# Layer norm's scale and bias moved from the reader of the residual rows to their writer, with the bias added by accumulating transfers

## The chip, the cores and the metric

One core of one Trainium2 chip. The metric is the device time of one execution in microseconds (us); the lower, the better.

## What is computed

Four layers over a sequence of 1024 rows of 1024 float32 numbers. Two are hybrid layers (gated delta rule and gated linear attention); two more have an attention (neighbourhood attention in one, grouped-query attention in the other) and a mixture of 32 experts, of which each row takes two. Around each of the six sublayers stands the same frame, cut here to what the change touches:

```python
# hybrid layer
y = jnp.einsum("bte,ed->btd", o, w_out)
x = layer_norm(ALPHA * x + y, ln_g, ln_b)             # (x - mean) * rsqrt(var + eps) * g + b
# layer of the second block
x = layer_norm_2(ALPHA * x + (1 + g1) * (attention @ w_o), ln_g[i, 0], ln_b[i, 0])
h = x * (1 + sc2) + sh2
y = hierarchical_moe(h, ...)
x = layer_norm_2(ALPHA * x + (1 + g2) * y, ln_g[i, 1], ln_b[i, 1])
```

So each normalised row xhat is wanted as a residual, ALPHA * (xhat * g + b), and after the attention sublayers also as the experts' input, xhat * g' + b' with g' = g * (1 + sc2) and b' = b * (1 + sc2) + sh2.

## The kernel before

The rows are cut into 8 tiles of 128 rows (128 x 1024 float32, 512 KB). The kernel is written as many chains (Python generators) with priorities; a list scheduler in the kernel's own code, `Flow`, replays them against modelled clocks and so fixes the order of the instructions on every engine. Nearly all instructions therefore carry the line of the helper that records them, L72; transfers that SyncE (SP) issues carry L185. Working memory is an arena of 47 slots of 128 x 1024.

`out_proj_ln` (called by each hybrid layer and each attention) multiplies the mixer's output with the output weights, tile by tile, adds the residual tile, which `Rows.tile` loads, and calls `finish`: the row statistics and `normalise`, then `Rows.put`, which stores the tile, and `post`. In the hybrid layers `post` transposes the tile for the next layer; in the second block it computes the router's logits, and the normalisation is part of it. For the second block this stage is called the mid stage here, of layer 0 and of layer 1. After its last tile come some hundred small VectorE (DVE) operations, the routing, then an extra block of experts and the experts' loop: per block of rows a gather by an indirect transfer that GpSimd (POOL) issues from the rows of h in DRAM, the three weight matrices, which SP loads, and a scatter that POOL issues and that adds its rows onto Y in DRAM. Each matrix is split in a high and a low part by ScalarE (ACT) and DVE. Layer 0's experts end in `moe_ln`: the second normalisation, a store of the rows, and `N.post`, which feeds the next attention and uses POOL for 64 small subtractions.

`Rows` is the description of such stored rows. Its buffers: xb0 and xb1 after the hybrid layers, xb2 and xb3 for h (x_mid) of layers 0 and 1, Y0 and Y1 for the residual onto which the experts' rows are added, xb4 after layer 0's experts. In `order` listings xb0 is xb_84, xb1 xb_85, xb2 xb_86, xb3 xb_87, xb4 xb_88.

What stands in them differs. xb0, xb1 and xb4 hold xhat; whoever reads a tile multiplies by ALPHA * g and adds ALPHA * b, two POOL operations on 128 x 1024 (`affine`). Y is written with scale and bias already applied (`early=True`): `put` does the same two POOL operations and then stores. For h `put` does a multiplication and an addition on DVE and then stores. The last two tiles of Y are held back until the routing is done (`mid.late`). `prepare` loads g and b at the start of `out_proj_ln`, scales them on ACT and, for h, makes g' and b' with one DVE and three POOL operations.

Of the kernel before, what the change touches and what calls it, by code (L numbers as in the profile page):

```python
# [14 lines left out]
ALU = mybir.AluOpType  # L15
# [17 lines left out]
class Event:  # L33
    def __init__(self):
        self.t, self.value = None, None
# [1435 lines left out]
class Rows:  # L1471
# [1 line left out]

    def __init__(self, x, g=None, b=None, early=False, also=None, mod=None):
        self.x, self.g, self.b, self.early, self.also, self.mod = x, g, b, early, also, mod
        self.rows, self.late = [], None

    def prepare(self, K, user, write=False):  # L1480
        if self.g is None or self.early != write:
            return
        for v in (self.g, self.b):
            r, t = yield from load_rows(K, user, v)
            yield from K.F.until(t)
            K.F.scalar.activation(r.f, r.f, AF.Copy, scale=ALPHA)
            self.rows.append(r)
        if self.mod is not None:
            P = K.F.gpsimd
            sc, t = yield from load_rows(K, user, self.mod[0])  # L1490
            sh, t = yield from load_rows(K, user, self.mod[1])
            g = yield from K.A.take(user)
            yield from K.F.until(t)
# [4 lines left out]
            K.A.give(sh)  # L1498
            self.rows += [g, sc]

    def affine(self, K, x, fast=0):

        P, V = K.F.gpsimd, K.F.vector
        (V if fast > 1 else P).tensor_mul(x.f, x.f, self.rows[0].f)
        (V if fast > 0 else P).tensor_add(x.f, x.f, self.rows[1].f)

    def put(self, K, x, t, user):

        V = K.F.vector
        if self.mod is not None:  # L1510
# [12 lines left out]

    def tile(self, K, x, t):

        F = K.F
        e = F.dma(x.f, self.x[t * 128:(t + 1) * 128, :])
        yield from F.until(e)
        if self.rows:
            self.affine(K, x)  # L1530
        elif not self.early:
            F.scalar.activation(x.f, x.f, AF.Copy, scale=ALPHA)

    def leave(self, K):
        K.A.give(*self.rows)
        self.rows = []


def out_proj_ln(K, oT, outs, wout, rows, eps, after, post, user, prio, freed=None):
# [32 lines left out]
    def finish(t, x):  # L1572
        if t > 1:
            yield posts[t - 2]
        if eps is not None:
            normalise(K, x.f, eps)
        if not after.early:
            yield from after.put(K, x, t, user)
        yield
        yield from post(t, x)  # L1580
        if after.early:
            yield from after.put(K, x, t, user)
        A.give(x)

# [49 lines left out]
        A.give(*o.done.value)  # L1634
    for e in posts:
        yield e
    rows.leave(K)
    after.leave(K)


# [1153 lines left out]
def moe_ln(K, l, Y, last, hold, there, x_out, N, user, prio):  # L2794
# [13 lines left out]
    def one(t, x, e):  # L2808
# [32 lines left out]
    if N is None:  # L2841
# [8 lines left out]
    for e in done:  # L2850
        yield e
    A.give(*hold.half[1].value)
    if N is None:
        A.give(gt, bt)

# [40 lines left out]
def block_2_layer(K, l, X, rows, x_mid, x_out, N, prio):  # L2896
# [21 lines left out]
    mid = Rows(Y, I["ln_g_2"][l, 0], I["ln_b_2"][l, 0], early=True, also=x_mid, mod=mod)  # L2918
    mid.late = M.routed
# [6 lines left out]
def whole(tc, I, O):  # L2926
    with ExitStack() as ctx:
        K = setup(ctx, tc, I)
        setup_2(K)
        xb = [K.dram.tile([S, D], F32, name=f"xb{i}") for i in range(5)]  # L2930

        def main():
            rows, X = yield from first_block(K, I["x"], xb[0:2])
            g, b = I["ln_g_2"][0, 1], I["ln_b_2"][0, 1]
            N = Next(K, "cols2", 0, g, b, 1)
            N.pool = True
            K.A.leave(N.X.user)
            yield from block_2_layer(K, 0, X, rows, xb[2], xb[4], N, 300)
            yield from block_2_layer(K, 1, N.X, Rows(xb[4], g, b), xb[3], O[0], None, 600)

        K.F.spawn(main(), 0)
        K.F.spawn(modulation(K, 90), 145)
        K.F.run()
# [37 lines left out]
```

## Time and profile before

| | |
|---|---|
| Runs | 4152.09, 4154.63, 4155.9 us; median 4154.63 |
| The profiled execution | 4151.23 us, its span 4149.4 us |
| TensorE (PE) busy | 3854.3 us, 93% of the span |
| DVE busy | 3207.2 us, 77% |
| ACT busy | 2194.5 us, 53% |
| POOL busy | 919.6 us, 22% |
| Mean granted TensorE clock | 0.957 of full speed |
| Transfers that SP issues (queue q1) | 644.95 MB |
| Transfers that POOL issues (queue q0) | 33.15 MB |

The profile is one execution. Busy times are sums over the instructions of an engine, so a share of 93% is a mean over stages: some have PE busy throughout, in others PE waits. The stages by time: the hybrid layers to about 1760, the first attention's end and layer 0's mid stage 1795 to 2030, layer 0's experts 2035 to 2640, their end 2639 to 2697, the second attention to 3373, layer 1's mid stage 3373 to 3451, then layer 1's experts.

### The profile page before, as it was taken

The numbers are of one execution on the slowest core, as the hardware profiler recorded it, in microseconds if no ns is written. First come the engines' busy times: TensorE is split into PE (matmuls) and PEld (weight loads), VectorE is DVE, ScalarE is ACT, GpSimd is POOL, SyncE is SP. The second block draws the span as 40 slices with busy tenths as digits, with TensorE's granted clock in tenths as the row PEclk, the third lists the DMA queues.
The fourth block names the chain that finished last, engine by engine and source line by source line (L and its number), as shares of the span: only waits on it lengthen the run. The fifth ranks groups of instructions, "written<-read, shape, count | busy, mean of one in ns | idle before, by whom it ended". The sixth has DMA issues, their size and how long they took to land. (4 is left out here: it accounts for less than half of the span.)

```text
span 4149.4 us, 62801 instructions
## 1 busy us (share of the span) xinstructions
PE 3854.3 (93%) x23000; PEld 3149.1 (76%) x23000; DVE 3207.2 (77%) x5956; ACT 2194.5 (53%) x3931; POOL 919.6 (22%) x638
## 2 busy tenths in 40 slices
PE   7999999999999999979799999889999886999997
PEld 6888788788887777757577777687777775777775
DVE  7787766775777788776789989766657786898898
ACT  4333335433334545441377767667779613777674
POOL 1111100220213233345322221310001251222212
PEclk9999999999999999988799999899999986999998
DMA  4232323111213433243699999400001235999994
GB/s 152 75 100 85 103 77 105 42 38 52 54 57 114 143 120 121 93 135 121 238 354 367 369 367 376 148 11 21 17 25 65 93 111 214 359 367 376 370 362 180
DMA packets 338766, 682.15 MB, mean 164 GB/s; under 512 B 59956, under 2 KB 190702, under 8 KB 338452
## 3 DMA queue, kind: packets, MB, share of 16 engines
q1 hardware_dynamic: 320020, 644.95, 43.2%
q0 software_dynamic: 18432, 33.15, 3.2%
q8 instruction: 182, 2.98, 0.3%
q14 instruction: 132, 1.08, 0.1%
HBM read 625.89 MB, written 86.08 MB: 172 GB/s over the span
## 5 line engine op out<-in xcount | busy, mean ns | idle before, releaser
L72 PE MATMUL banks<-slot 128*128 128x512 f32 (+8 forms) x18258 | 3249.2, 345 | 81.5 <-DVE slot L72 45.5
L72 PEld LDWEIGHTS banks<-slot 128*128 128x128 f32 (+5 forms) x18258 | 2565.3, 178 | 624.9 <-issue 93.1
L72 DVE TENSOR_TENSOR slot<-slot 128x1024 fp32r<-128x1024 f32 (+14 forms) x1417 | 1378.0, 1001 | 129.1 <-ACT slot L72 65.5
L72 ACT ACTIVATE slot<-slot 128x1024 fp32r<-128x1024 f32 (+5 forms) x1011 | 996.5, 1019 | 663.4 <-PE banks L72 233.3
L72 ACT ACTIVATE slot<-banks 128x512 f32<-128x512 f32 (+8 forms) x1124 | 548.7, 510 | 678.0 <-PE banks L72 611.5
L72 POOL TENSOR_TENSOR slot<-slot 128x384 f32<-128x384 f32 (+3 forms) x270 | 451.9, 1692 | 1373.2 <-PE banks L72 404.0
L72 PE MATMUL banks<-c,slot 128*128 128x128 f32 (+2 forms) x3484 | 514.5, 285 | 110.8 <-DVE slot L72 41.8
L72 PEld LDWEIGHTS banks<-c,slot 128*128 128x128 f32 (+1 forms) x3484 | 425.7, 158 | 207.5 <-issue 51.5
L72 DVE TENSOR_TENSOR slot<-banks,slot 128x512 fp32r<-128x512 f32 (+4 forms) x622 | 364.9, 608 | 164.2 <-PE banks L72 92.0
L72 ACT ACTIVATE slot<-slot,small 128x1024 f32<-128x1024 f32 (+1 forms) x292 | 265.9, 923 | 197.5 <-DVE small L72 193.7
L72 DVE COPY slot<-banks 128x512 f32<-128x512 f32 (+6 forms) x406 | 220.2, 551 | 103.4 <-PE banks L72 78.3
L72 POOL MEMSET slot<- 128x1024 f32 (+1 forms) x70 | 66.6, 956 | 836.9 <-PE banks L72 413.8
L72 POOL DMA_INDIRECT Y<-slot,small x62 | 143.5, 2314 | 258.9 <-DVE slot L72 206.3
L72 ACT ACTIVATE slot<-banks,small 128x1024 f32<-128x1024 f32 x140 | 156.5, 1121 | 66.7 <-DVE small L72 58.4
L72 DVE TENSOR_REDUCE small<-banks 128x1 f32<-128x1024 f32 x128 | 154.3, 1220 | 45.2 <-PE banks L72 44.3
L72 PE MATMUL banks<-slot,small 128*128 128x512 f32 (+2 forms) x388 | 158.0, 544 | 19.5 <-ACT small L72 10.2
L72 DVE SCALAR_TENSOR_TENSOR slot<-slot,c_act 128x1024 f32<-128x1024 f32 x84 | 120.0, 1430 | 29.2 <-DMA slot<-in_ada_w 24.2
L72 DVE SCALAR_TENSOR_TENSOR small<-small 128x1 f32<-128x1 f32 (+3 forms) x590 | 128.7, 223 | 12.8
L72 PE MATMUL banks<-small,slot 128*128 128x128 f32 (+1 forms) x576 | 107.0, 301 | 25.0 <-DVE small L72 21.2
L72 ACT ACTIVATE small<-banks 128x64 f32<-128x64 f32 (+2 forms) x289 | 78.0, 274 | 96.9 <-PE banks L72 90.7
L72 DVE TENSOR_TENSOR slot<-slot,banks 128x512 f32<-128x512 f32 (+4 forms) x110 | 72.2, 664 | 69.9 <-PE banks L72 69.0
L72 PEld LDWEIGHTS banks<-small,slot 128*128 128x128 f32 (+1 forms) x576 | 83.6, 200 | 40.4 <-DVE small L72 16.8
(129 smaller groups left out, 1732.7 us busy)
## 6 DMA issues: line engine op xcount, KB each, us to landing
slot<-in_moe_w_up SPq DMA_DIRECT2D x260, 512.0 KB
slot<-in_moe_w_down SPq DMA_DIRECT2D x260, 512.0 KB
slot<-in_moe_w_gate SPq DMA_DIRECT2D x260, 512.0 KB
slot<-in_ada_w SPq DMA_DIRECT2D x96, 512.0 KB
slot<-in_w_in SPq DMA_DIRECT2D x56, 512.0 KB
xb<-slot SPq DMA_DIRECT2D x40, 512.0 KB
slot<-xb SPq DMA_DIRECT2D x24, 512.0 KB
slot<-in_na_w_qkv SPq DMA_DIRECT2D x24, 512.0 KB
```

The lines of the kernel that those rows point to most:

```text
L72: r = real(*a, **k)
```

## The change

The writer now applies scale and bias everywhere, and the reader only loads.

- `prepare` is spawned beside `out_proj_ln` (and beside `moe_ln` of layer 0) and no longer runs ahead of it. It loads g and b, for h also the modulation, which it folds with four DVE operations; ACT scales by ALPHA. Then `preset` fills the destination in DRAM with the bias: the slot that holds b in every row is written to each of the 8 tiles' places by a plain SP transfer.
- `put` multiplies xhat by the scale on DVE, into a slot of its own, and POOL issues a transfer with `accum_op=ALU.add` that adds the slot onto the preset rows. In the mid stages it does so twice per tile, for h and for Y.
- `affine`, `early` and `mid.late` are gone.

In numbers of instructions, from the two listings: POOL loses 86 operations on 128 x 1024 (16 in the second hybrid layer, 35 in each mid stage; the 35 of layer 0 are 16 for the read of xb1, 16 for Y and 3 in `prepare`) and issues 56 accumulating transfers more. DVE loses 34 such operations and gets 64 (56 products and 8 in `prepare`). SP loses 56 stores, and gets 56 presets and 2 more loads of b.

```diff
-            K.F.vector.tensor_scalar(sc.f, sc.f, 1.0 / ALPHA, 1.0 / ALPHA, op0=ALU.mult, op1=ALU.add)
-            P.tensor_mul(g.f, self.rows[0].f, sc.f)
-            P.tensor_mul(sc.f, self.rows[1].f, sc.f)
-            P.tensor_add(sc.f, sc.f, sh.f)
...
-    def affine(self, K, x, fast=0):
-        P, V = K.F.gpsimd, K.F.vector
-        (V if fast > 1 else P).tensor_mul(x.f, x.f, self.rows[0].f)
-        (V if fast > 0 else P).tensor_add(x.f, x.f, self.rows[1].f)
...
+                V.scalar_tensor_tensor(sh.f, b.f, 1.0, sh.f, op0=ALU.mult, op1=ALU.add)
+                V.tensor_mul(b.f, b.f, sc.f)
+                V.tensor_add(sh.f, sh.f, b.f)
+                V.scalar_tensor_tensor(sc.f, sc.f, 1.0, g.f, op0=ALU.add, op1=ALU.mult)
+                self.preset(K, self.also, sh)
+                self.to.append((self.also, sc))
+            t = F.dma(b.f, rows_of(self.b, 0, D))
+            yield from F.until(t)
+        with F.aside():
+            for a in (g, b):
+                F.scalar.activation(a.f, a.f, AF.Copy, scale=ALPHA)
+            self.preset(K, self.x, b)
+            self.to.append((self.x, g))
+        F.set(self.ready)
+
+    def preset(self, K, dst, b):
+        for t in range(NT):
+            K.F.dma(dst[t * 128:(t + 1) * 128, :], b.f)
+        K.A.give(b)

     def put(self, K, x, t, user):
-            with K.F.aside():
-                V.tensor_mul(h.f, x.f, self.rows[2].f)
-                V.tensor_add(h.f, h.f, self.rows[3].f)
-                K.F.dma(self.also[t * 128:(t + 1) * 128, :], h.f)
-                K.A.give(h)
-        if self.late is not None and t >= NT - 2:
-            yield self.late
-        with K.F.aside():
-            if self.early:
-                self.affine(K, x)
-            K.F.dma(self.x[t * 128:(t + 1) * 128, :], x.f)
+        yield self.ready
+        for dst, r in self.to:
+            h = yield from K.A.take(user)
+            with F.aside():
+                F.vector.tensor_mul(h.f, x.f, r.f)
+                F.gpsimd.dma_start(dst[t * 128:(t + 1) * 128, :], h.f, accum_op=ALU.add)
+            def sent(h=h):
+                yield from F.until(F.last(h.f))
+                K.A.give(h)
+            F.spawn(sent(), 0)

     def tile(self, K, x, t):
         e = F.dma(x.f, self.x[t * 128:(t + 1) * 128, :])
         yield from F.until(e)
-        if self.rows:
-            self.affine(K, x)
-        elif not self.early:
+        if self.g is None:
             F.scalar.activation(x.f, x.f, AF.Copy, scale=ALPHA)
...
 def out_proj_ln(K, oT, outs, wout, rows, eps, after, post, user, prio, freed=None):
-    yield from rows.prepare(K, user)
-    yield from after.prepare(K, user, True)
+    F.spawn(after.prepare(K, user), prio - 0.45)
...
 def moe_ln(K, l, Y, last, hold, there, x_out, N, user, prio):
-        F.dma(x_out[t * 128:(t + 1) * 128, :], x.f)
+        if N is None:
+            F.dma(x_out[t * 128:(t + 1) * 128, :], x.f)
+        else:
+            yield from x_out.put(K, x, t, user)
...
+    if N is not None:
+        F.spawn(x_out.prepare(K, user), prio)
```

POOL, layer 0's mid stage up to the first gather (`slot<-xb_86`), as one piece of the difference:

```order
-L72 TENSOR_TENSOR slot<-slot 128x384 x8
-L72 TENSOR_TENSOR slot<-slot 128x1024 x3
-L72 TENSOR_TENSOR slot<-slot 128x384 x6
-L72 TENSOR_TENSOR slot<-slot 128x1024 x2
-L72 TENSOR_TENSOR slot<-slot,small 128x384 x2
-L72 TENSOR_TENSOR slot<-slot 128x1024 x26
...
+L72 DMA xb_86<-slot 128x1024 x2
+L72 DMA Y_15128<-slot 128x1024 x2
+L72 DMA xb_86<-slot 128x1024
+L72 DMA Y_15128<-slot 128x1024
...
 L72 DMA slot<-xb_86,small 128x1024 x2
```

POOL no longer works on the tiles there; in front of the gather stand 16 accumulating transfers, the two of the last tile directly in front of it.

DVE at the end of the first attention, where layer 0's mid stage begins; before:

```order
L72 TENSOR_TENSOR slot<-slot 128x1024
L72 TENSOR_SCALAR slot<-slot,small 128x384
L72 TENSOR_TENSOR slot<-slot 128x1024 x6
L72 COPY slot<-banks 128x384 x2
L72 COPY slot<-banks 128x4x8x16
```

and with the change:

```order
L72 COPY slot<-banks 128x384
L72 TENSOR_SCALAR slot<-slot,small 128x384
L72 COPY slot<-banks 128x384
L72 TENSOR_TENSOR slot<-slot 128x1024 x7
L72 ISA slot,small<-banks,slot 128x384
```

The run of wide operations that splits the output weights is still in one piece, and a copy out of the accumulation banks that stood behind it now stands ahead.

SP behind the extra block of layer 0's experts, before:

```order
L185 DMA slot<-in_moe_w_up 128x1024 x4
L185 DMA slot<-in_moe_w_down 128x1024 x4
L185 DMA slot<-in_moe_w_gate 128x1024 x4
```

and with the change:

```order
L185 DMA slot<-in_moe_w_up 128x1024 x2
L185 DMA slot<-in_moe_w_down 128x1024 x2
L185 DMA slot<-in_ln_g 128x1024
L185 DMA slot<-in_ln_b 128x1024
L185 DMA slot<-in_moe_w_down 128x1024 x2
L185 DMA slot<-in_moe_w_gate 128x1024
L185 DMA xb_88<-slot 128x1024 x8
L185 DMA slot<-in_moe_w_gate 128x1024 x3
```

Two loads and the eight presets of xb4 now stand between the first weights of the experts' loop.

## Rows read from the trace of the kernel before

**Rows 1.** The page of the profile: the span, and its part 1.

```profile
span 4149.4 us, 62801 instructions
...
PE 3854.3 (93%) x23000; PEld 3149.1 (76%) x23000; DVE 3207.2 (77%) x5956; ACT 2194.5 (53%) x3931; POOL 919.6 (22%) x638
```

**Rows 2.** Windows over five stages; columns stand in the first line.

```profile
core 0: us, PE busy (x) PEld busy (x) DVE busy (x) ACT busy (x) POOL busy (x), PEclk, DMA share, GB/s
740.00:780.00 40.00, 33.72 (x155) 27.44 (x155) 32.74 (x60) 19.27 (x28) 13.93 (x8) 0.91 0.05 14
1710.00:1760.00 50.00, 49.71 (x280) 39.62 (x278) 32.36 (x92) 23.72 (x56) 14.26 (x16) 1.00 0.16 56
2178.00:2593.00 415.00, 414.54 (x1861) 330.10 (x1860) 372.16 (x384) 299.96 (x363) 96.21 (x64) 1.00 0.99 370
2639.00:2697.00 58.00, 43.88 (x233) 35.77 (x232) 45.88 (x165) 43.50 (x128) 28.25 (x64) 0.82 0.35 130
3373.00:3451.00 78.00, 46.61 (x275) 40.99 (x273) 72.03 (x185) 12.30 (x19) 39.21 (x17) 0.68 0.45 171
```

**Rows 3.** Groups by shape, POOL: 1795 to 2030, then 3350 to 3455.

```profile
L72 POOL TENSOR_TENSOR slot<-slot 128x1024 f32<-128x1024 f32 x35 | 98.2, 2810 | 73.9 <-DVE slot L72 44.1 <-DMA slot<-xb 27.0 <-issue 1.3
...
L72 POOL TENSOR_TENSOR slot<-slot 128x1024 f32<-128x1024 f32 x18 | 50.3, 2795 | 51.0 <-DVE slot L72 35.8 <-DMA slot<-xb 14.6
```

**Rows 4.** Groups by shape, DVE in the experts' loop, 2178 to 2593.

```profile
L72 DVE TENSOR_TENSOR slot<-slot 128x1024 fp32r<-128x1024 f32 x246 | 289.8, 1219 | 3.2 <-ACT slot L72 0.4 <-PE banks L72 0.3
```

**Rows 5.** Groups by shape, DVE in layer 1's mid stage, 3350 to 3455.

```profile
L72 DVE TENSOR_TENSOR slot<-slot 128x1024 f32<-128x1024 f32 x16 | 34.9, 2198 | 0.0
```

**Rows 6.** Groups by shape, DVE in layer 0's mid stage, 1795 to 2030.

```profile
L72 DVE TENSOR_TENSOR slot<-slot 128x1024 f32<-128x1024 f32 x24 | 36.0, 1503 | 6.7 <-DMA slot<-in_na_w_o 3.6 <-ACT slot L72 3.0
L72 DVE TENSOR_TENSOR slot<-slot 128x1024 fp32r<-128x1024 f32 x8 | 17.4, 2208 | 0.7 <-ACT slot L72 0.7
L72 DVE TENSOR_TENSOR slot<-slot 128x896 fp32r<-128x896 f32 x8 | 13.7, 1721 | 10.5 <-DMA Y<-slot 6.3 <-PE banks L72 3.8 <-ACT slot L72 0.4
```

**Rows 7.** Timelines of DVE, then PE: start, length, operation, idle before.

```profile
1841.88 16.20 DVE L72 TENSOR_TENSOR slot<-slot 128x1024 f32<-128x1024 f32 x6
...
1858.60 5.63 PE L72 MATMUL banks<-slot 128*64 128x128 f32 x40 [15.62 <-DVE slot L72]
```

**Rows 8.** Timeline, end of the routing of layer 1: DVE, then POOL.

```profile
3434.92 1.23 DVE L72 TENSOR_TENSOR slot<-slot 128x1024 f32<-128x1024 f32 x1
...
3437.34 2.31 DVE L72 TENSOR_SCALAR slot<-slot 128x8 f32<-128x8 f32 x1
...
3439.69 0.23 DVE L72 TENSOR_TENSOR slot<-slot 128x64 f32<-128x64 f32 x1
...
3440.20 1.99 DVE L72 TENSOR_TENSOR slot<-slot 128x64 f32<-128x64 f32 x1
...
3450.75 1.08 POOL L72 DMA_INDIRECT slot<-xb,small  x1 [8.64 <-DVE small L72]
```

**Rows 9.** Groups by shape, DVE where xb4 is read, 3264 to 3300.

```profile
L72 DVE TENSOR_TENSOR slot<-slot 128x896 fp32r<-128x896 f32 x4 | 8.4, 2159 | 0.0
L72 DVE TENSOR_TENSOR slot<-slot 128x1024 fp32r<-128x1024 f32 x3 | 7.1, 2366 | 0.0
```

**Rows 10.** The tile Y: POOL's scatters, then all its transfers' landings.

```profile
L72 POOL DMA_INDIRECT Y<-slot,small x62: 2281/2314/2466, 2062.9 to 4085.6; - x62
...
DMA to landing us min/median/max: 4.8/9.7/10.8
```

**Rows 11.** The page's part 3: DMA queues.

```profile
q1 hardware_dynamic: 320020, 644.95, 43.2%
q0 software_dynamic: 18432, 33.15, 3.2%
```

**Rows 12.** Waits of SP's queue in layer 0's experts, 2035 to 2593.

```profile
SPq L185 <- DMA slot<-in_moe_w_down: 130.8, 99, 3.6
...
SPq L185 <- PE banks L72: 86.9, 101, 7.3
```

More of the change, by code (lines that the diff above doesn't have):

```diff
@@ L1471 @@
 class Rows:
[L1476 to L1481, printed above, removed]
-            return
[L1483 to L1487, printed above, removed]
-        if self.mod is not None:
[L1489 to L1493, printed above, removed]
-            K.F.vector.tensor_scalar(sc.f, sc.f, 1.0 / ALPHA, 1.0 / ALPHA, op0=ALU.mult, op1=ALU.add)
-            P.tensor_mul(g.f, self.rows[0].f, sc.f)
-            P.tensor_mul(sc.f, self.rows[1].f, sc.f)
-            P.tensor_add(sc.f, sc.f, sh.f)
-            K.A.give(sh)
-            self.rows += [g, sc]
@@ L1501, in affine, with __init__, prepare @@
-    def affine(self, K, x, fast=0):
-        P, V = K.F.gpsimd, K.F.vector
-        (V if fast > 1 else P).tensor_mul(x.f, x.f, self.rows[0].f)
-        (V if fast > 0 else P).tensor_add(x.f, x.f, self.rows[1].f)
+    def __init__(self, x, g=None, b=None, also=None, mod=None):
+        self.x, self.g, self.b, self.also, self.mod = x, g, b, also, mod
+        self.to, self.ready = [], Event()
+    def prepare(self, K, user):
+        F, V = K.F, K.F.vector
+        if self.g is None:
+            F.set(self.ready)
+            return
+        r = []
+        for v in (self.g, self.b) + (self.mod or ()):
+            r.append((yield from load_rows(K, user, v)))
+        for _, t in r:
+            yield from F.until(t)
+        g, b = r[0][0], r[1][0]
+        if self.mod is not None:
+            sc, sh = r[2][0], r[3][0]
+            with F.aside():
[6 more added lines that the diff above has]
+            t = F.dma(b.f, rows_of(self.b, 0, D))
+            yield from F.until(t)
+        with F.aside():
[3 more added lines that the diff above has]
+            self.to.append((self.x, g))
+        F.set(self.ready)
@@ L1517, in put @@
-        if self.late is not None and t >= NT - 2:
-            yield self.late
-        with K.F.aside():
-            if self.early:
-                self.affine(K, x)
-            K.F.dma(self.x[t * 128:(t + 1) * 128, :], x.f)
+            with F.aside():
+                F.vector.tensor_mul(h.f, x.f, r.f)
+                F.gpsimd.dma_start(dst[t * 128:(t + 1) * 128, :], h.f, accum_op=ALU.add)
+            def sent(h=h):
+                yield from F.until(F.last(h.f))
+                K.A.give(h)
@@ L1528, in tile @@
         yield from F.until(e)
-        if self.rows:
-            self.affine(K, x)
-        elif not self.early:
+        if self.g is None:
             F.scalar.activation(x.f, x.f, AF.Copy, scale=ALPHA)
     def leave(self, K):
-        K.A.give(*self.rows)
-        self.rows = []
+        K.A.give(*(r for _, r in self.to))
+        self.to = []
 def out_proj_ln(K, oT, outs, wout, rows, eps, after, post, user, prio, freed=None):
@@ L1576, in finish @@
             normalise(K, x.f, eps)
-        if not after.early:
             yield from after.put(K, x, t, user)
@@ L1580, in finish @@
         yield from post(t, x)
-        if after.early:
+        if eps is None:
             yield from after.put(K, x, t, user)
@@ L1636, in out_proj_ln @@
         yield e
-    rows.leave(K)
     after.leave(K)
@@ L2852, in moe_ln @@
     A.give(*hold.half[1].value)
+    if N is not None:
+        x_out.leave(K)
     if N is None:
@@ L2917, in block_2_layer @@
     mod = K.mod_d[l][4 * D:5 * D], K.mod_d[l][3 * D:4 * D]
-    mid = Rows(Y, I["ln_g_2"][l, 0], I["ln_b_2"][l, 0], early=True, also=x_mid, mod=mod)
-    mid.late = M.routed
+    mid = Rows(Y, I["ln_g_2"][l, 0], I["ln_b_2"][l, 0], also=x_mid, mod=mod)
     user.peak = 39
@@ L2937, in main @@
             K.A.leave(N.X.user)
-            yield from block_2_layer(K, 0, X, rows, xb[2], xb[4], N, 300)
-            yield from block_2_layer(K, 1, N.X, Rows(xb[4], g, b), xb[3], O[0], None, 600)
+            after = Rows(xb[4], g, b)
+            yield from block_2_layer(K, 0, X, rows, xb[2], after, N, 300)
+            yield from block_2_layer(K, 1, N.X, after, xb[3], O[0], None, 600)
         K.F.spawn(main(), 0)
```

3 lines of the change are left out of this document (1 added, 2 removed).

## The prediction

> **What bounds the kernel now.** I begin with the page: PE is busy for 93% of a span of 4149.4 us [rows 1]. That is a mean, so the next view is the windows, cut by stage [rows 2]. In the experts' loop (2178 to 2593) PE is busy for 414.54 of 415 us: nothing taken from another engine can shorten it, and the transfers, at a share of 0.99, have no room. The end of the second hybrid layer (1710 to 1760) is full of PE as well, 49.71 of 50. Layer 1's mid stage (3373 to 3451) is not: PE 46.61 of 78, DVE 72.03. There DVE sets the pace, and half of its time is not its own work. The groups by shape show that: a DVE operation with two slots as inputs takes 1.22 us on 128 x 1024 in the experts' loop, where POOL does none of `affine`'s [rows 4]; in this stage, where POOL runs 18 operations of 2.80 us [rows 3], 16 of the same size take 2.20 us each [rows 5]. In layer 0's mid stage POOL runs 35 of 2.81 us [rows 3], and three DVE groups are long as well [rows 6]. So POOL's row operations, off the path by themselves, stretch DVE's where DVE is the path. The timelines show one such place whole: six wide DVE operations take 16.20 us, and PE stands idle for 15.62 until DVE's next copies come [rows 7].
>
> **Layer 1's mid stage.** POOL's 18 operations go, DVE's 16 stay 16: a product and an addition for h become two products. The excess is 16 x (2.198 - 1.219) = 15.7 us [rows 4, 5]. DVE is busy for 72.03/78 of the stage [rows 2], so 14.5 of it lie on the path. In the routing two operations of a few columns take 2.31 and 1.99 us beside Y's last two tiles, where one of this kind takes 0.23 [rows 8]: 3.9 us more, all of it on the path to the gather. Together 18 us gained. Bounds: 0, if PE's work or the transfers end last instead, and 78 - 46.6 = 31, if only PE's work were left.
>
> **Layer 0's mid stage.** The excess in the three groups is 24 x 0.284 = 6.8, 8 x 0.99 = 7.9 and 8 x 0.65 = 5.2 us (the last against 1.219 x 896/1024 = 1.07) [rows 4, 6]: 19.9 us, most of it beside PE's work. On the path lies the gap: six operations at 1.22 us are 7.3 us, so 8.9 of the 16.20 go [rows 7]; the change leaves this run of DVE in one piece (seven). With the routing's 3.9, taken as in layer 1 (an estimate), I gain 13. Bounds: 4, if the gap only moves to a later run of DVE, and 24, the whole excess.
>
> **The read of xb4.** Seven DVE operations are long beside `affine`: 3 x 1.15 + 4 x 1.09 = 7.8 us [rows 4, 9]. Nothing shows that DVE ends that stage alone: bounds 0 and 7.8, and I take 3.
>
> **The hybrid layers.** `affine` also leaves the second hybrid layer, and 8 DVE products (8 x 1.22 = 9.8 us) come into the end of each. At the end of the second, PE hides them [rows 2]: nothing, and up to 5 us lost if its 0.3 us of room were no cover for a late transpose. At the end of the first (740 to 780) PE and DVE are busy for 33.72 and 32.74 of 40 us [rows 2]; the transposes don't wait for the product, only for the engine behind it: 1 us lost, bounds 0 and 5.
>
> **The end of layer 0's experts.** Here 8 products (9.8 us) come to a DVE that is busy for 45.88 of 58 us, and 8 issues to a POOL that is busy for 28.25 with subtractions on which the next products of PE rest [rows 2]. POOL's scatter with addition takes 2.31 us to issue [rows 10], its plain gather 1.08 [rows 8]: 8.6 to 18.5 us on POOL, which still fits into the stage. Neither engine becomes full, but the tile's chain passes through both. I take a third to a quarter of the 28 us together: 6 us lost, bounds 2 and 12. What speaks against the change here: POOL's issues could be held up by DVE. The scatters are issued beside a DVE that is busy for 372 of 415 us [rows 2], and none of 62 takes over 2.47 us [rows 10]. The Trainium skill's page SBUF — State Buffer, section 🔬 SBUF: two separate sides, says that a transfer issued from GpSimd starves for descriptors while VectorE holds the shared port; its section on the wrong bandwidth intuition gives some 3.1 us instead of 0.62. By that figure the 8 issues would be 24.8 us (an estimate), and my 6 would be 8; the rows here show nothing so long, and the sum goes by them.
>
> **The weight stream of layer 0's experts.** Ten transfers of 0.524 MB (two loads, eight presets) stand between the first weights on SP's queue, 10 x 0.524 MB at 370 GB/s = 14.2 us [rows 2]. Is this stream hidden? SP waits longer for transfers that hold a slot (130.8 us for one matrix alone) than for PE to free one (86.9) [rows 12], so it runs not far ahead. Yet PE is busy throughout. I take 3.5 us lost, bounds 0 and 14.2. The presets of the mid stages replace stores one for one, in a stage with DMA at 0.45 [rows 2]: nothing, covered by that idle half; behind them on SP's queue stand the first weights, and these are in place long before the gather.
>
> **The gather.** It must wait until both accumulating transfers of the last tile have landed; before, its own rows were a plain store. The scatter, of the same kind and on average 33.15 MB/128 = 0.26 MB [rows 11], lands in 9.7 us, at most 10.8 [rows 10]. A tile is twice that. By the queue's mean a tile's transfer costs 0.524 x (0.032 x 4149.4 us/33.15 MB) = 2.1 us of all 16 engines, a plain one 1.5 [rows 11], so I add 3 us of transfer: 12 to 13 us. The room: the last tile's product for h ends at 3436.15, and the gather goes out at 3450.75 [rows 8]; of these 14.6 us the routing's 3.9 fall away, which leaves 10.7. So each of the two gathers is 2 us late, 4 lost; bounds 0 and 9.7 for each, the last if one more scatter's time lies ahead of it.
>
> **The sum.** Gained 18 + 13 + 3 = 34; lost 1 + 6 + 3.5 + 4 = 14.5; net 19.5. The profiled execution of 4151.2 us becomes 4131.7. The median of the runs lies 3.4 above that execution, so the predicted time is **4135 us**. A measurement of this kernel tells about 0.2%, 8.3 us, from no change: faster is below 4146.3, slower above 4162.9.
>
> **The rivals.** *The whole excess comes through.* If layer 0's mid stage gives 24 us and layer 1's 24 (its small operations are stretched too), the xb4 read 6, and the losses halve to 7, the net is 47; with half of these extras 33. That is 4108 to 4122, middle 4115. For it: DVE is the stage's engine, at 72.03 of 78. Against: in layer 0 only one gap of this size stands between PE's work. 13%.
>
> *Gained in the mid stages, given back at the experts.* The ten transfers cost their 14.2 us because the weights have no room at a DMA share of 0.99 [rows 2], the end of layer 0's experts costs 10, the gathers 6: 34 - 31 = 3, which is 4152. For it: SP's waits [rows 12]. Against: PE's 414.54 of 415 says that the stream still arrives in time. 18%.
>
> *Slower: the gather waits for the accumulating transfers.* If these queue behind one another (16 per stage on one queue) and behind the weights that SP has begun to load, the last lands L us after its product, and each stage loses L - 10.7. Without the gathers the net gain is 23.5, so it is used up at L = 22.5; over 0.2% is lost from L = 26.6. At L = 30, three of the landings of [rows 10], it is 38.6 lost against 23.5 gained: 4154.6 + 15 = 4170. For it: POOL's issues are in order, and a transfer that reads and writes DRAM has no row of this size. Against: 8 tiles in 78 us come some 10 us apart, and DMA is at 0.45. 14%. That the change doesn't do what it says is no case here: the listing shows all 86 POOL operations gone.
>
> **How the numbers follow.** The forecast has 55%, with 4125 to 4143 as its own range. The rival that gains more has 13%; both lie below 4146.3, so faster has 68%. Given back is the 18% of the same, the late gather the 14% of slower. The range of 8 in 10 reaches from 4105, below the rival that gains more, to 4160, past the one that gives all back; what it leaves out is the late gather and a few per cent below.
>
> **What would show it.** Right: wide POOL operations only outside the mid stages, DVE's of 128 x 1024 at about 1.22 us there, PE's gap of 15.62 down to some 7, the stage from the last attention product to layer 1's gather shorter by 16, and PE still busy throughout the experts' loop. Wrong: a gather that a transfer releases, tens of us after the last DVE product; PE gaps in the first rounds of layer 0's experts, where the presets stand; an end of layer 0's experts over 12 us longer, with POOL's issues well above 2.3 us each; or mid stages as long as before, with another engine full.

## The result, and the profile after

The changed kernel takes 4097.66 us (median of 4 runs, 4093.67 to 4102.15), the kernel before 4155.26 in the same session: a ratio of 0.9866, 95% interval 0.9848 to 0.9885. Run once more beside later experiments it took 4109.41 (4094.53 to 4112.13), a ratio of 0.9883 (0.985 to 0.9916); so two sessions of one kernel can lie 12 us apart. Against the forecast of 4135 and its range from 4105 the sign is right and the size is not: 58 us gained, and not 20.

The page of the changed kernel, span, engines and POOL's DMA queue:

```profile
span 4098.2 us, 62930 instructions
...
PE 3826.4 (93%) x23000; PEld 3123.1 (76%) x23000; DVE 3145.8 (77%) x5986; ACT 2207.1 (54%) x3931; POOL 756.7 (18%) x608
...
q0 software_dynamic: 26496, 62.51, 7.4%
```

PE is busy for 28 us less than before [rows 1] with the same 23000 instructions, POOL for 163 us less; POOL's queue now moves 62.51 MB and not 33.15 [rows 11].

To see where 51 us of span went, cut both traces where the same number of matmuls is done. Windows of the kernel before (length, then PE, PEld, DVE, ACT, POOL busy with their counts, the granted clock, DMA share, GB/s): the end of the first hybrid layer, layer 0's mid stage up to its first gather (905 matmuls), layer 1's with the read of xb4 ahead (825):

```profile
680.00:800.00 120.00, 112.41 (x520) 91.94 (x519) 91.53 (x245) 56.15 (x110) 19.34 (x12) 0.96 0.21 60
1795.00:2026.00 231.00, 175.47 (x905) 142.94 (x903) 171.64 (x408) 50.00 (x88) 108.97 (x47) 0.81 0.36 128
3264.00:3450.00 186.00, 145.12 (x825) 122.07 (x824) 147.41 (x303) 34.82 (x48) 83.79 (x32) 0.84 0.36 128
```

The changed kernel: the same three (518, 905 and 820 matmuls), and then pieces of layer 0's experts and of their end, which answer to two of [rows 2]:

```profile
676.00:808.00 132.00, 112.97 (x518) 90.84 (x517) 94.81 (x256) 61.43 (x130) 25.48 (x19) 0.92 0.30 65
1815.00:1994.00 179.00, 154.73 (x905) 125.89 (x904) 138.54 (x408) 50.69 (x87) 29.31 (x26) 0.93 0.75 221
3234.00:3386.00 152.00, 134.69 (x820) 113.65 (x818) 102.15 (x307) 32.35 (x45) 15.80 (x18) 0.92 0.77 218
2145.00:2560.00 415.00, 410.18 (x1837) 324.98 (x1836) 371.26 (x381) 304.27 (x359) 98.26 (x62) 1.00 0.99 370
2606.00:2664.00 58.00, 39.52 (x196) 30.16 (x194) 55.82 (x171) 38.33 (x108) 32.67 (x55) 0.82 0.54 113
```

Read as a ledger, with the starts and lengths of these windows: layer 0's mid stage begins 20 us later than before (1815 against 1795), 12 of them lost at the end of the first hybrid layer (132 against 120). It is 52 us shorter (179 against 231). Layer 1's window begins 30 earlier, so layer 0's experts and their end gave 2 back. It is 34 shorter (152 against 186). The end comes 51 earlier, so layer 1's experts and what follows gave 13 back. 20 - 52 + 2 - 34 + 13 = -51. Eight of the 51 are luck of the execution: after 3500 matmuls, at about 560 us, where the work is still almost the same, the profiled execution of the changed kernel is 8.0 us ahead of the kernel before. The profiled execution of its repeat is 0.2 us behind there and ends 39 us ahead.

In layer 0's mid stage the 905 matmuls kept PE busy for 175.47 us before and 154.73 now: a granted clock of 0.81 against 0.93, 21 us. The other 31 are PE's idle time. DVE does 408 operations in both, in 171.64 and 138.54 us.

DVE's groups of the changed kernel, two rows of layer 1's stage behind those of layer 0's; they answer to [rows 5, 6]:

```profile
L72 DVE TENSOR_TENSOR slot<-slot 128x1024 f32<-128x1024 f32 x25 | 29.9, 1218 | 2.8 <-ACT slot L72 2.8
...
L72 DVE TENSOR_TENSOR slot<-slot 128x1024 fp32r<-128x1024 f32 x8 | 9.6, 1224 | 2.5 <-ACT slot L72 2.4
L72 DVE TENSOR_TENSOR slot<-slot 128x896 fp32r<-128x896 f32 x8 | 8.6, 1084 | 2.1 <-ACT slot L72 2.1
...
L72 DVE TENSOR_TENSOR slot<-slot 128x1024 f32<-128x1024 f32 x18 | 21.6, 1221 | 3.8 <-ACT slot L72 3.6
L72 DVE SCALAR_TENSOR_TENSOR small<-small 128x1 f32<-128x1 f32 x56 | 10.9, 195 | 1.9
```

All wide operations stand at the undisturbed duration of [rows 4]. The last row is the surprise. The same one-column operations of layer 1's stage, before, then two runs of seven of them, and what POOL does beside the second run:

```profile
L72 DVE SCALAR_TENSOR_TENSOR small<-small 128x1 f32<-128x1 f32 x56 | 18.9, 338 | 1.7
...
3344.64 1.50 DVE L72 SCALAR_TENSOR_TENSOR small<-small 128x1 f32<-128x1 f32 x7
3354.53 4.89 DVE L72 SCALAR_TENSOR_TENSOR small<-small 128x1 f32<-128x1 f32 x7
...
3353.69 4.87 POOL L72 TENSOR_TENSOR slot<-slot 128x1024 f32<-128x1024 f32 x2 [14.61 <-DMA slot<-xb]
```

They read two operands of 4 bytes in each partition and still lost 8 us in all, but not evenly: 51 of the 56 took at most 224 ns, as 55 do in the changed kernel, and five took 1.45 to 2.26 us. Each of these five ended 15 to 23 ns after a product of POOL that had begun before it. In layer 0's stage none took over 0.87 us, and their sum is nearly the same before and after, 11.0 and 10.8 us.

PE's gap behind the run of wide DVE operations in layer 0's mid stage, then its longest gap there, at the routing; then the way to layer 1's gather, DVE's last product but one and POOL's last two issues (start, length, idle before):

```profile
1847.12 0.90 PE L72 MATMUL banks<-c,slot 128*128 128x128 f32 x3 [5.80 <-DVE small L72]
...
1987.64 0.19 PE L72 MATMUL banks<-both,before_b 128*128 128x32 bf16 x1 [8.50 <-DVE both L72]
...
3374.13 1.23 DVE L72 TENSOR_TENSOR slot<-slot 128x1024 f32<-128x1024 f32 x1
...
3375.65 0.87 POOL L72 DMA_DIRECT2D xb<-slot  x1 [5.98 <-DVE slot L72]
3376.93 0.87 POOL L72 DMA_DIRECT2D Y<-slot  x1 [0.41 <-DVE slot L72]
3386.57 1.74 POOL L72 DMA_INDIRECT slot<-xb,small  x1 [8.78 <-DVE slot L72]
```

The gap at the routing, before:

```profile
2019.95 0.19 PE L72 MATMUL banks<-both,before_b 128*128 128x32 bf16 x1 [13.06 <-DVE both L72]
```

The gap of 15.62 us [rows 7] became one of 5.80, that of 13.06 one of 8.50. The gather is released by DVE, not by a transfer; the last accumulating transfer was issued 9.6 us before it.

### The profile page after: what moved, and what is told of

Same layout as the page of the kernel before. It is cut to its first block, busy times and chain, and to the rows that moved or that the text cites. A ratio compares the mean times of both kernels' runs of the same rounds, so it can differ in the third digit from the quotient of the medians.

```text
span 4098.2 us, 62930 instructions
## 1 busy us (share of the span) xinstructions
PE 3826.4 (93%) x23000; PEld 3123.1 (76%) x23000; DVE 3145.8 (77%) x5986; ACT 2207.1 (54%) x3931; POOL 756.7 (18%) x608
## 3 DMA queue, kind: packets, MB, share of 16 engines
q0 software_dynamic: 26496, 62.51, 7.4%
HBM read 626.94 MB, written 115.44 MB: 181 GB/s over the span
## 5 line engine op out<-in xcount | busy, mean ns | idle before, releaser
L72 PE MATMUL banks<-slot 128*128 128x512 f32 (+9 forms) x18258 | 3231.3, 343 | 81.9 <-ACT slot L72 55.6
L72 DVE TENSOR_TENSOR slot<-slot 128x1024 fp32r<-128x1024 f32 (+13 forms) x1445 | 1360.0, 964 | 245.1 <-ACT slot L72 168.2
L72 POOL TENSOR_TENSOR slot<-slot 128x384 f32<-128x384 f32 (+2 forms) x184 | 225.6, 1251 | 982.3 <-PE banks L72 416.8
L72 POOL DMA_DIRECT2D xb<-slot x40 | 35.1, 885 | 725.2 <-DVE slot L72 581.3
L72 DVE SCALAR_TENSOR_TENSOR small<-small 128x1 f32<-128x1 f32 (+3 forms) x590 | 120.1, 211 | 11.7
```

The lines of the kernel that those rows point to most:

```text
L72: r = real(*a, **k)
```

## The experiments

Several variants come from one file in which each buffer of rows can be switched between the old and the new manner (`old=True` brings back `affine`, the plain store and, for the mid stages, the hold on Y and the blocking preparation). For comparison, the two mid stages, cut in every trace from the same matmul (the 905th before layer 0's first gather, the 822nd before layer 1's) to the start of that gather: the length, PE's idle time in it and DVE's busy time, in us.

```text
kernel      layer 0: length, PE idle, DVE   layer 1: length, PE idle, DVE   median, all runs
before      231.1  55.3  171.7              186.4  41.6  147.8              4153 to 4156
changed     179.3  24.4  138.8              153.1  17.9  103.3              4097.7, 4109.4
e_dummy     209.4  42.3  168.6              179.6  39.0  137.8              4163.3
e_memset    179.3  24.8  139.8              149.4  15.3  103.8              4107.2
e_read      202.3  37.5  159.8              174.3  28.6  121.0              4136.7
e_write     213.1  36.0  161.6              161.1  22.5  117.6              4132.1
e_spawn     223.8  53.1  178.3              178.7  35.5  137.6              4152.5
e_dve       192.6  30.7  169.3              162.6  26.0  131.1              4101.1
e_plain2    179.4  23.7  138.7              147.2  14.5  103.2              4083.7
```

**e_dummy and e_memset: is it POOL's reading?** Both add POOL work to the changed kernel whose results nobody uses, in a small tile of its own; the order on the other engines stays, but for some twenty rows.

```diff
+def idle(K, x):                       # e_dummy
+    for _ in range(4):
+        K.nc.gpsimd.tensor_mul(K.idle, x.f[:, 0:448], x.f[:, 448:896])
+def idle(K, x):                       # e_memset
+    K.nc.gpsimd.tensor_mul(K.idle[:, 0:8], x.f[:, 0:8], x.f[:, 8:16])
+    for _ in range(10):
+        K.nc.gpsimd.memset(K.idle, 0.0)
...
+            if rows.reads:
+                idle(K, w[0])
             yield from rows.tile(K, x, t)
...
         yield self.ready
+        if self.mod is not None:
+            idle(K, x)
```

> The changed kernel with POOL work put back in both mid stages that nobody waits for: per tile four products of 448 columns beside the read of the residual tile and four beside the writes (64 per stage; 98 us of wide operations stood there before). The order on PE, DVE, ACT and SP stays that of the changed kernel but for some twenty rows. Theory P (POOL's row operations block DVE, PE starves, its clock falls; that is where the mid stages' gain of some 80 us came from): most of the gain goes again, 4130 to 4160 us, DVE's wide operations in the mid stages well above 1.22 us. Theory C (the chain of each tile became shorter: no two POOL operations between load and addition, prepare no longer ahead, Y not held back): within 8 us of the changed kernel's 4097.7.

> The control to e_dummy: the same places in POOL's order, but each group of four products is one product of 8 columns and ten fills of 448 columns, which write to SBUF and read nothing from it; POOL is about as long busy. Theory P (POOL's reads of SBUF block DVE's operations with two inputs there): within 10 us of the changed kernel's 4097.7, DVE's products at 1.22 us. Theory Q (what costs in e_dummy is POOL's queue: accumulating transfers issued late, slots held longer): as e_dummy, 4150 to 4165.

Measured: e_dummy 4163.34 us, ratio to before 1.0023 (1.001 to 1.0037): the time is that of the kernel before, and a little more. e_memset 4107.2, ratio 0.9898 (0.9857 to 0.9939): the gain stays. The groups of layer 0's mid stage, first e_dummy, then e_memset (both lines of POOL's added work and DVE's wide products):

```profile
L1476 POOL TENSOR_TENSOR idle<-slot 128x448 bf16<-128x448 f32 x64 | 101.0, 1578 | 31.0 <-ACT slot L72 27.5
L72 DVE TENSOR_TENSOR slot<-slot 128x1024 f32<-128x1024 f32 x25 | 37.4, 1515 | 2.0 <-ACT slot L72 2.0
```

```profile
L1477 POOL MEMSET idle<- 128x448 bf16 x160 | 82.7, 517 | 8.3
L72 DVE TENSOR_TENSOR slot<-slot 128x1024 f32<-128x1024 f32 x25 | 29.9, 1217 | 2.9 <-ACT slot L72 2.9
```

With 101.0 us of POOL's products DVE's take 1.515 us; with 82.7 us of its fills, 1.217. So it is POOL's reading of SBUF that stretches DVE's operations, not its being busy and not its queue. The Trainium skill, SBUF — State Buffer, section Who interferes with whom, says just this: a DVE instruction with two SBUF inputs contends with a GpSimd instruction that reads SBUF, not with one that only writes it. Both runs agree with it, 1.515 against 1.217 us.

In the mid stages, though, e_dummy takes back 30 us of 52 and 27 of 33, together 57 of 85, with DVE busy nearly as long as before. Some 28 us stay gained. No run says whether they have another source or whether the added products only meet DVE's work in other places than the old ones did. Nor is e_dummy quite without a wait: ACT waits for the added products for 19.9 us (two waits) in layer 0's stage, but PE's waits on ACT come to 3.9 us there, against 1.5 in the changed kernel.

**e_read and e_write: which side?** `mid` in the old manner and the rest new; and the reverse.

```diff
-OLD = ()
+OLD = ("mid",)                  # e_read
+OLD = ("xb0", "xb1", "xb4")     # e_write
```

> Mid stages write h and Y as before (POOL operations, plain stores, Y's last tiles held back, prepare ahead); xb0, xb1 and xb4 as in the changed kernel, so that the readers have no POOL operations. Theory P: read and write shares add up by their POOL time (16 of 35 operations each stage), so 0.45 of the mid stages' 80 us is gained and the losses outside (some 27 us) stay: 4142 to 4152. Theory C with the read side alone deciding: 4100 to 4110.

> Only the mid stages as in the changed kernel (presets, products, accumulating transfers); xb0, xb1 and xb4 as before, with the readers' POOL operations. Theory P: 0.55 of the mid stages' 80 us without the losses outside: 4105 to 4120. Theory C with the write side alone deciding: below 4090. If the read side decides: above 4135.

4136.71 us (0.9956, 0.9939 to 0.9973) and 4132.11 (0.9948, 0.9932 to 0.9964), both outside what theory P gave. In the mid stages the two sides add up. Readers: 28.8 and 12.1 us less than before; writers: 18.0 and 25.3; together 84, and the changed kernel has 51.8 + 33.3 = 85. Outside, e_read keeps the hybrid layers' loss and e_write the one in the experts' loops, so the medians show less.

**e_spawn: the preparation.** The kernel before, with both preparations beside the projection; readers and writers wait for theirs.

```diff
     if rows.old:
-        yield from rows.prepare_old(K, user)
+        F.spawn(rows.prepare_old(K, user), prio - 0.45)
     if after.old:
-        yield from after.prepare_old(K, user, True)
+        F.spawn(after.prepare_old(K, user, True), prio - 0.45)
```

> The kernel before with its two preparations beside the output projection and not ahead of it; POOL's row operations, stores and the hold on Y's last tiles stay. Theory C (the blocking preparation cost the mid stages their time): over 15 us faster than before. Theory P: within 8 us of before, 4147 to 4163.

4152.48 us, ratio 0.9992 (0.9972 to 1.0012): nothing in the whole. In its trace, an execution of 4170.93 us, the two mid stages are 7.3 and 7.7 us shorter than before, and the way to layer 0's stage 31 us longer. So the preparation may account for part of the 28 us that e_dummy leaves; one trace doesn't show it.

**e_dve: the work stays, the engine changes.** The kernel before, with `affine` on DVE.

```diff
     def affine(self, K, x):
-        P = K.F.gpsimd
+        P = K.F.vector
```

> The kernel before with the row operations of readers and of Y on DVE and not on POOL (three POOL operations of each preparation stay). Every instruction's work is as before, the engine alone differs. Theory P: DVE gets 32 operations of 1.22 us in each mid stage, 39 us, and loses some 30 to 37 us of stretching there; so within 25 us of before, 4130 to 4180, and DVE's wide operations at 1.22 us. Without blocking (rival) it would be 39 us per mid stage slower where DVE sets the pace: above 4200.

4101.1 us (4087.16 to 4108.08), ratio 0.986 (0.9834 to 0.9886): as fast as the changed kernel, by one word. Both theories expected less. DVE's wide operations in layer 0's mid stage:

```profile
L72 DVE TENSOR_TENSOR slot<-slot 128x1024 f32<-128x1024 f32 x56 | 69.1, 1260 | 3.7 <-DMA slot<-in_na_w_o 3.7
```

There are 56 now where [rows 6] has 24, at 1.260 and not 1.503. The work added to DVE is 32 x 1.22 = 39 us, and the stage is still 38 us shorter than before, with DVE busy for 169.3 us against 171.7. So the long chain of presets, products and accumulating transfers is not what the gain rests on, and the sum of DVE's busy time is not what sets the stage's length. What sets it is where PE waits: its idle time fell from 55.3 to 30.7 us. That POOL's two slow steps also left each tile's chain, in this run as in the changed kernel, is a rival that e_dve doesn't tell from the stretching; e_dummy, which stretches DVE's operations without those steps, takes back only 57 of the 85. In the mid stages e_dve gains 62 us of the 85; it has no wait on the gate in layer 1's experts (see e_pool).

**e_plain2: what the addition costs.** The order of every engine is that of the changed kernel; the transfers overwrite, so the bias is missing from the rows.

```diff
-                F.gpsimd.dma_start(dst[t * 128:(t + 1) * 128, :], h.f, accum_op=ALU.add)
+                F.gpsimd.dma_start(dst[t * 128:(t + 1) * 128, :], h.f)
```

> The changed kernel with every engine's order unchanged, but the POOL transfers of the rows overwrite and do not add; the bias of the layer norms is left out of the rows that way (the presets are still written). Theory A (adding in the transfer costs nothing that PE sees: landing 5.6 us, and the gathers wait for the routing): within 6 us of 4097.7. Rival (the read and write of DRAM delays slots or gathers): over 10 us faster.

4083.71 us (4082.2 to 4087.36; 0.9832, 0.9811 to 0.9852), some 14 below the changed kernel and 26 below its repeat: theory A falls, though the intervals of the ratios still touch (0.9848 for the changed kernel). POOL's transfers of rows (count, KB each, us to landing), the changed kernel and then this one:

```profile
xb<-slot POOLq DMA_DIRECT2D x40, 512.0 KB, 5.6
...
Y<-slot POOLq DMA_DIRECT2D x16, 512.0 KB, 8.8
```

```profile
xb<-slot POOLq DMA_DIRECT2D x40, 512.0 KB, 3.9
...
Y<-slot POOLq DMA_DIRECT2D x16, 512.0 KB, 5.5
```

An addition lands 1.7 to 3.3 us later. In layer 0's mid stage nothing follows from it. Layer 1's is 6 us shorter, 147.2, but 149.4 in e_memset, which adds in its transfers. Most of the time is saved in the hybrid layers: 6 us of PE's idle time at the end of the first, where slots come free sooner, and 5.5 at the start of the first attention.

**e_xb0old, in_rows, e_best12: the hybrid layers.** The changed kernel loads the second hybrid layer's first weights late. Its SP queue, the first split that waits for them, PE's gap behind it, and SP's waits from 600 to 700 us (total, times, longest):

```profile
699.35 7.83 SPq L185 DMA_DIRECT2D slot<-in_w_in  x3
...
710.45 1.06 ACT L72 ACTIVATE slot<-slot 128x1024 fp32r<-128x1024 f32 x1 [7.64 <-DMA slot<-in_w_in]
...
718.44 1.22 PE L72 MATMUL banks<-slot 128*128 128x512 f32 x2 [11.69 <-ACT slot L72]
...
SPq L185 <- DMA xb<-slot: 15.0, 2, 7.6
```

The same load before:

```profile
679.28 1.01 SPq L185 DMA_DIRECT2D slot<-in_w_in  x2
```

Every product holds a slot until its transfer has landed, and SP has none for the weights. e_xb0old stores xb0 as before (`OLD = ("xb0",)`). in_rows multiplies xb0, xb1 and xb4 in place, behind the transposes. e_best12 is in_pool12 (below) with xb0 as before and its reader on DVE.

```diff
+def INPLACE(rows):                       # in_rows
+    return rows.mod is None
...
-            h = yield from K.A.take(user)
+            h = x if INPLACE(self) and dst is self.x else (yield from K.A.take(user))
...
             normalise(K, x.f, eps)
-            yield from after.put(K, x, t, user)
         yield
         yield from post(t, x)
-        if eps is None:
-            yield from after.put(K, x, t, user)
-        A.give(x)
+        yield from after.put(K, x, t, user)
+        if not INPLACE(after):
+            A.give(x)
```

> The changed kernel with only the first hybrid layer's rows (xb0) as before: xhat stored plainly, the second layer's reader multiplies and adds on POOL. Theory S (the slots that products hold until their accumulating transfers land delay the next layer's weight loads on SP, and PE waits 11.7 us at 718): 12 to 16 us faster than the changed kernel, 4082 to 4086, and no wait of PE above 4 us between 690 and 740. Rival (the POOL operations come back at the read in the second layer and cost there what they cost in the mid stages): within 5 us of 4097.7.

> The changed kernel with xb0, xb1 and xb4 multiplied in place after the transposes; nothing of the planner's constants changed, and the order in layer 1's experts' loop is that of the changed kernel. Theory S (slots held by the accumulating transfers delay the next layer's weights): 12 to 17 us faster than the changed kernel, 4080 to 4086. Rival (what PE gains there it loses at the next wait): 4094 to 4101.

> As in_pool12, but xb0 is stored plainly as xhat, as before, and the second hybrid layer's reader multiplies and adds on DVE, not on POOL. Theory H (the changed kernel's loss in the hybrid layers comes from the slots of the first layer's accumulating transfers; e_xb0old gave none of it back because POOL's reading returned in the second layer): within 4 us of in_pool12, since in place already freed the slots. Rival (any transfer of rows with addition in the first layer costs, in place too): 5 to 12 us faster than in_pool12.

e_xb0old: 4108.21 us (0.9882, 0.9861 to 0.9903), no gain. in_rows: 4091.36 (4089.57 to 4110.14; 0.9863, 0.9832 to 0.9894), its profiled run 4089.57. e_best12: 4088.16 (0.9841, 0.9813 to 0.9868), not faster than in_pool12. PE's waits from 640 to 780 us in in_rows:

```profile
PE banks L72 <- DVE slot L72: 6.1, 2, 5.3
PE banks L72 <- ACT slot L72: 1.0, 2, 0.5
```

and in the repeat of the changed kernel, where the wait on the split comes again:

```profile
PE banks L72 <- ACT slot L72: 14.7, 3, 11.3
```

So the slots cause that wait: 14.7 us, twice, and 1.0 in place. e_plain2, with the changed kernel's order and landings 1.7 us sooner, has 9.3. The profiled execution of in_rows reaches layer 0's mid stage at 1796.5 us, that of the changed kernel at 1814.8. That this is worth 12 us or more in the whole time the medians don't show: 4091 against 4098 and 4109.

Why e_xb0old gained nothing is open in part. It passes the end of the first layer (matmuls 4300 to 4500) in 56.1 us, the changed kernel in 68.2, so the 12 us are there. Its profile loses 6 of them again where a stretch of 20 us at half clock follows a gap of 2 us at 930; the kernel before has the same gap and loses less. It loses 9 more between matmuls 8000 and 8500, where xb0 is read on POOL again: 120.6 us, with PE idle for 10.2, against 112.0 and 2.2. e_best12, which reads on DVE there, takes 111.8; but the kernel before, with its POOL operations, takes no more, 110.7. POOL's reading alone is therefore not shown as the cause.

**e_pool, in_pool12 and the repeats: the order in layer 1's experts.** The changed kernel's loop has a wait of PE per expert that the kernel before has not. PE's waits there (total, times, longest), before and changed:

```profile
PE banks L72 <- ACT small L72: 0.5, 2, 0.2
```

```profile
PE banks L72 <- ACT small L72: 9.9, 21, 0.5
```

The engine is ACT: the gate's activation stands behind one more split of weights. The planner's arithmetic decides that, so one constant was changed.

```diff
-        return 1.04        # what the planner reckons for the issue of a POOL transfer
+        return 0.87        # e_pool; with in_rows e_inpool
+        return 1.2         # with in_rows: in_pool12
```

> The changed kernel with one constant of the planner changed: what it reckons for the issue of a POOL transfer, 1.04 us, is 0.87, as measured on the accumulating ones. POOL's and SP's order stay; on ACT the activation of the gate in layer 1's experts' loop comes one split earlier, which is the order that the kernel before had. Theory O (that order costs PE 0.47 us per expert, 10 us in all): 4085 to 4091 us, and PE's waits on that activation fall from 9.9 us to under 1. Rival (PE waits for something else in the same place, the weights for one): 4094 to 4101.

> As e_pool, and the rows xb0, xb1 and xb4 are multiplied in place, after the transposes, so that their accumulating transfers hold no slot of their own. Theory S (slots held by these transfers delay the next layer's weights on SP; 11 us of PE's idle time at 718 and some 5 at 1390): 4070 to 4080 us. Rival (SP's order still has those weights behind the last tile of the input, so PE waits as long): as e_pool, within 5 us.

> As in_rows, and the planner reckons 1.2 us for the issue of a POOL transfer (not 1.04), which brings back, in layer 1's experts' loop, the repeating order on ACT and DVE that the kernel before had, the weights' splits four ahead of the gate. Theory O (it is this lead that decides PE's wait per expert: 0.47 us at a lead of 0, 3.1 at 1, none at 4): PE's waits in that loop under 1.5 us, 4068 to 4078. Rival (the wait has another cause, such as the gather): within 4 us of in_rows or slower.

> in_pool12 once more, beside the changed kernel on the same chip: 12 to 20 us faster than that one.

> The changed kernel once more, for the comparison on one chip: 4093 to 4104 us; PE's 0.47 us per expert in layer 1's loop again, and its idle time at the end of the first hybrid layer again 10 us or more above the kernel before, if both are matters of the order and not of this execution.

e_pool: 4209.51 us, 112 slower than the changed kernel, with POOL's and SP's order as it was; e_inpool: 4207.25. in_pool12: 4080.9 (0.9829, 0.9795 to 0.9863), again 4083.01 beside 4109.41 for the changed kernel. The waits on the gate, e_pool and in_pool12:

```profile
PE banks L72 <- ACT small L72: 60.7, 20, 5.3
```

```profile
PE banks L72 <- ACT small L72: 0.2, 1, 0.2
```

Theory O had the place right and e_pool's direction wrong: a truer constant made the wait 3 us per expert, a less true one removed it. From layer 1's gather to the end PE idles for 78 us more in e_pool than in the changed kernel and loses 36 more at half clock, which accounts for the 112. in_pool12 is the fastest version found, 15 to 26 us below the changed kernel, although its layer 0 mid stage is longer, 194.9 and 187.5 us in its two profiles. The repeat of the changed kernel, at 4109.41, lies above the 4104 expected of it; its trace has the 9.9 us on the gate again, and the wait at the end of the first hybrid layer.

## Why the prediction was wrong

**The bound and the mechanism: right, and shown for two thirds of the mid stages' gain.** POOL's row operations stretched DVE's, PE waited for DVE, and without them DVE's wide operations stand at 1.22 us. e_dummy and e_memset show that POOL's reading costs 57 of the 85 us. That these operations were "off the path by themselves" is not shown: for the other 28 us it stays open whether POOL's slow steps in each tile's chain, the preparation that ran ahead or the new order counted, or whether e_dummy's products stretch less than the old ones.

**Layer 0's mid stage: 13 forecast, 52 measured. This is the step that failed.** "19.9 us, most of it beside PE's work. On the path lies the gap" took one gap out of a stage, with the routing, and called the rest covered. The two places that it counted came nearly as forecast: the gap gave 9.8 us for 8.9, the wait at the routing 4.6 for 3.9. Two terms were missing. First, the other waits: of PE's idle time 31 us went, so 17 more than in these two places (PE's waits on DVE's slots came to 29.0 us before and to 1.2 now). Second, the granted clock: at 0.81 before and 0.93 now the same 905 matmuls take 21 us less. The sum had no line for what PE's waits cost at half clock. DVE's excess was larger than counted as well: its 408 operations became 33 us shorter, and not 19.9 + 3.9. Narrower operations that the sum left out make up the rest, those of 128 x 384 for one; here before and after:

```profile
L72 DVE TENSOR_SCALAR slot<-slot,small 128x384 f32<-128x384 f32 x16 | 9.9, 626 | 0.0
```

```profile
L72 DVE TENSOR_SCALAR slot<-slot,small 128x384 f32<-128x384 f32 x16 | 6.6, 426 | 0.0
```

**Layer 1's mid stage and the read of xb4: 21 forecast, 34 measured.** The same two terms: PE's busy time is 10 us shorter and its idle time 24; DVE's busy time is 45 shorter (303 and 307 operations), where the sum counted 15.7 + 3.9 + 7.8 = 27. Eight of these 45 are the one-column operations.

**The gather: 2 us late each forecast, not late at all.** The term took the scatter's 9.7 us and added 3; the rows land in 5.6 and 8.8, and DVE releases the gather. POOL's issue was mis-sized as well, in the same direction:

```profile
L72 POOL DMA_DIRECT2D xb<-slot x40: 857/866/1213, 632.6 to 3375.7; - x40
```

It takes 0.87 us, below the lower end taken, 1.08. The Trainium skill, SBUF — State Buffer, section 🔬 SBUF: two separate sides, lets such issues starve for descriptors while VectorE runs an operation in a 2-port mode; the prediction weighed that at 3.1 us each. Nothing of it shows in this trace: none of the 40 issues took over 1.213 us. The slower rival, which rested on late landings, had no ground.

**The experts of layer 0 and their end: 9.5 us lost forecast, 2 measured.** PE is busy for 410.18 of 415 us, so the presets and the loop's order cost under 5 us, where the term had 3.5. The end of the stage lost little, though DVE is busy for 55.82 of 58. The term itself was misreckoned: a third to a quarter of its 28 us is 7 to 9, and not 6.

**The hybrid layers: 1 us lost forecast, 20 measured.** The step "the transposes don't wait for the product, only for the engine behind it" looked at engines and not at slots. Some 12 lie at the end of the first layer, where PE waits for weights that found no slot. Another 7 lie around 1391, at the start of the first attention, where PE has a gap of 9.91 us; in_rows idles there as long, so its cause stays open. The 20 are net of the 8 us of luck in the first 560: the repeat, without them, arrives at layer 0's mid stage 29 us late.

**Layer 1's experts and the end: nothing forecast, 13 lost.** Some 10 of it is the wait on the gate. The prediction took a loop that is full of PE as safe from the change; a different start of the loop gave it another repeating order.

The rival in which "the whole excess comes through" was nearest, at 4115, and its conditions (24 us in each mid stage) were still too small. That it came near is in part luck: by the ledger the mid stages gained 86 us, and 35 were lost elsewhere.

## What to carry to other kernels

Where GpSimd works on rows beside a VectorE that TensorE waits for, don't price the stretch on the wide operations and the visible gap alone: narrow ones, down to one column, can wait for the end of a GpSimd product too. Add what TensorE then loses at half clock: cut the trace by equal numbers of matmuls and read idle time and busy time apart. The sum of VectorE's busy time is no forecast of the stage (e_dve). Then try the cheapest way to take the reading off GpSimd; one word (e_dve) gave as much as the change. In a kernel whose order a planner writes, look at the repeating order of the longest loop after every edit, since there one place in a queue times 32 is worth more than most edits.

## What the runs showed of the hardware

- GpSimd's products hold up VectorE's operations of one column: five of 56 took 1.45 to 2.26 us and ended 15 to 23 ns after the product, the others at most 0.22. Fills by GpSimd left VectorE's wide products at 1.217 us.
- An accumulating transfer of 512 KB lands in 5.6 to 8.8 us, a plain one by the same queue in 3.9 to 5.5, and its issue takes 0.87 us. With the same bytes, GpSimd's queue takes 7.4% of the 16 DMA engines' span with the additions and 5.0% without (e_plain2). The page counts as much read from HBM with the additions as without, 626.94 MB.
- Executions of one kernel differ in where the clock is at half. The first 560 us, whose work is almost the same in all of them, cost 18.0 to 31.8 us of PE's busy time in that way over the profiles here (busy time at half clock, halved). That is as much as several of the effects sought, so sessions of four runs leave 10 us open.
